# The first group of a two-level MLP product: two products of the second group taken into it, and buffers and steps moved to make room

## The chip, the cores and the metric

The kernel runs on one core of one Trainium2 chip. The metric is the device time of one execution in microseconds (us). A core has five engines that each work through their own list of instructions in order: TensorE (PE, matmuls and their weight loads), VectorE (DVE), ScalarE (ACT), GpSimd (POOL, here mostly a queue that issues DMAs) and SyncE (SP, a queue that issues DMAs). They meet at semaphores only: an instruction whose operand is not ready stands at the head of its engine's list, and all that is behind it waits too. Matmul results land in PSUM, eight banks of 128 x 512 float32; everything else lives in SBUF, in rooms that pools hand out by tag.

## The reference

One block of a hybrid encoder on a sequence of 512 rows and 2048 columns, in float32:

```python
h = rmsnorm(x, norm_mix_pre);  proj = h @ w_in                      # 2048 x 5120
mix = concat(pool_mixer(proj[:, :1024]), hgrn2(proj[:, 1024:])) @ w_out
x = x + rmsnorm(mix, norm_mix_post)
h = rmsnorm(x, norm_mlp_pre)
ff = square(relu(h @ w_mlp_in)) @ w_mlp_out                         # 2048 x 8192, 8192 x 2048
out = x + rmsnorm(ff, norm_mlp_post)
```

## The kernel before, in words

**Float32 by halves.** Every float32 operand is split in two: a high half that ACT writes by a cast, and a low half, which is the operand minus the high half and which DVE writes. A product is then three matmuls: high by high, high by low, low by high. A weight tile of 512 x 512 (one DMA of 1 MB) is split in two pieces of 128 x 1024 each, on ACT (line 863, results named `mh`) and DVE (line 864, `ml`). An operand of the activations is split the same way (`split_in`, lines 895 and 896, results named `a`).

**Stages.** The input projection (`pj`, ten groups of four units) with the pooling and the recurrence between its matmuls; the out projection (`om`, four groups); the first MLP product; the second MLP product. In the projection's first group, the sum of squares of x is turned into a row `rbc` that scales every result: DVE writes a diagonal tile `rb_dg`, PE spreads it by one matmul (`rb_ps`, line 129), ACT copies it (line 130), and then the results of the group can leave their banks.

**The first MLP product** takes 2 x 2 blocks by seven products in place of eight (numbered 1 to 7, done in the order 1, 2, 5, 3, 6, 7, 4). `slots` lists (group, product, half): eight groups of 1024 columns, seven products, two halves of the depth, so 112 slots. Each slot multiplies one weight tile (split while the slot before runs) with one activation operand. Products 5, 3, 6 and 7 need sums of activation blocks (`s1`, `s2`, `s3`, `s7`, line 899) before their operands can be split. The operands are kept for all groups, so only the first group, slots 0 to 13, makes them, and it does so while it runs: transposing the out projection's rows on PE (`feed_in`, result `fps`, moved out of PSUM on ACT at line 924 or on DVE at line 928), forming sums and splitting. The table `plan` says which of these steps stand ahead of a slot's matmuls and which in their middle. The rows themselves come from the out projection: `residual_task` scales a tile of 128 rows, adds x (line 779) and stores it, and `norm2_task` (lines 791 to 802) squares it for the second norm. A little clock (`clock.tick`, once per block or slot) runs such tasks after a count of ticks.

The first group runs *narrow*: 48 matmuls of 256 columns per slot, in single banks (`mi`, line 1035), since four of the eight banks serve the transposes. Later groups run *wide*: 16 matmuls of 512 columns (high and low operand side by side, line 1020) and 16 of 256 (line 1023), in `ps`.

**Weights.** Product 1, 5, 6 and 4 use a tile X, product 2, 3 and 7 a tile YZ; after a split the next tile is added onto the old one by an accumulating DMA on POOL (line 870), or a new one is loaded by SP (lines 847 and 853). `YZ0` takes the room that the norm weight `wpost` held during the out projection.

Lines of the loop that set the order in a slot:

```python
w_split_all(k + 1)
for f in before:
    f()
clock.tick()
products_in(k, hook)
evac_in(k, 1)
```

The split of the next slot's weight thus stands first in the lists of ACT and DVE, and the operand splits of the plan behind it.

## Time and profile before

| | us |
|---|---|
| median of 3 runs (lowest, highest) | 1971.12 (1970.82, 1973.6) |
| the profiled execution: time, span | 1971.38, 1969.7 |
| PE busy | 1944.2 |
| DVE busy | 1286.0 |
| ACT busy | 837.7 |
| input projection's first 100 us: PE without work from 20 to 100 us | 1.0 |
| first MLP group, slots 0 to 13, by the first and the last matmul's start | 699.3 to 798.0 |
| PE without work from 699.3 to 757.2 us | 7.5 |
| granted PE clock from 748.1 to 754.3 us | 0.50 |

The profile gives, for each engine, when an instruction began, how long it took and what ended the wait ahead of it. Starts matter more than durations: the duration of a matmul or of a DVE step overlaps the next one, so the pace is the distance between starts. PE counts as busy while a matmul is in its pipeline; whether it runs at full speed is told by the granted clock alone.

### The profile page before, as it was taken

The numbers are of one execution on the slowest core, as the hardware profiler recorded it, in microseconds if no ns is written. First come the engines' busy times: TensorE is split into PE (matmuls) and PEld (weight loads), VectorE is DVE, ScalarE is ACT, GpSimd is POOL, SyncE is SP. The second block draws the span as 40 slices with busy tenths as digits, with TensorE's granted clock in tenths as the row PEclk, the third lists the DMA queues.
The fourth block names the chain that finished last, engine by engine and source line by source line (L and its number), as shares of the span: only waits on it lengthen the run. The fifth ranks groups of instructions, "written<-read, shape, count | busy, mean of one in ns | idle before, by whom it ended". The sixth has DMA issues, their size and how long they took to land.

```text
span 1969.7 us, 24368 instructions
## 1 busy us (share of the span) xinstructions
PE 1944.2 (99%) x10008; PEld 1657.4 (84%) x10008; DVE 1286.0 (65%) x1420; ACT 837.7 (43%) x1000; POOL 145.1 (7%) x227
## 2 busy tenths in 40 slices
PE   9999999999999999999999999999999999999996
PEld 7888888888888889988888888888888888888885
DVE  5647443754632387566765766677778878878877
ACT  6222232223232275444444444445544444444454
POOL 1000000000000010111111011011010010010110
PEclk9999999999999999999999999999999999999998
DMA  7231222211343377889889888898897897897896
GB/s 310 86 107 65 86 69 103 86 65 65 118 192 107 118 206 193 214 216 220 213 213 216 229 210 211 223 241 245 209 251 222 200 236 229 210 227 219 219 227 134
DMA packets 56063, 354.98 MB, mean 180 GB/s; under 512 B 6032, under 2 KB 7056, under 8 KB 18064
## 3 DMA queue, kind: packets, MB, share of 16 engines
q0 software_dynamic: 24912, 162.54, 39.4%
q1 hardware_dynamic: 30752, 190.37, 26.5%
q8 instruction: 78, 1.28, 0.2%
q10 hardware_dynamic: 288, 0.52, 0.1%
q14 instruction: 33, 0.27, 0.0%
HBM read 328.24 MB, written 25.17 MB: 179 GB/s over the span
## 4 chain that ended last, share of the span: by engine, by line
PE 93%; DVE 2%; ACT 2%; DMA 1%; issue 1%; SPq 0%; DVEq 0%; ACTq 0%
PE pj L243 20%; PE ps L1020 18%; PE al L1236 17%; PE ga L1236 13%; PE ps L1023 10%; PE om L243 9%; PE mi L1035 3%; PE lps L610 2%; DMA xt<-in_x_t 1%; DVE ml L864 1%; DMA wr<-in_w_in 0%; ACT xrow L405 0%; ACT mh L863 0%; PE po L673 0%; DVE a L896 0%
## 5 line engine op out<-in xcount | busy, mean ns | idle before, releaser
L1020 PE MATMUL ps<-a,mh 128*128 128x512 f32 x1568 | 378.4, 391 | 0.0
L1020 PEld LDWEIGHTS ps<-a,mh 128*128 128x128 f32 x1568 | 286.7, 188 | 54.9 <-issue 0.3
L1236 PE MATMUL al<-mh,o 128*128 128x512 f32 x1024 | 316.9, 389 | 0.0
L863 ACT CAST mh<-X 128x1024 fp32r<-128x1024 f32 x176 | 180.2, 1053 | 209.7 <-PE ps L1020 87.5
L863 ACT CAST mh<-YX 128x1024 fp32r<-128x1024 f32 x176 | 180.5, 1054 | 157.4 <-PE al L1236 44.6
L864 DVE TENSOR_TENSOR ml<-X,mh 128x1024 fp32r<-128x1024 f32 x176 | 207.4, 1220 | 57.7 <-ACT mh L863 57.4
L1236 PE MATMUL ga<-mh,o 128*128 128x512 f32 x768 | 237.7, 389 | 0.0
L243 PE MATMUL pj<-xT,wh 128*128 128x512 f32 x760 | 236.2, 392 | 0.0
L864 DVE TENSOR_TENSOR ml<-YX,mh 128x1024 fp32r<-128x1024 f32 x176 | 207.4, 1220 | 35.2 <-ACT mh L863 35.1
L1236 PEld LDWEIGHTS al<-mh,o 128*128 128x128 f32 x1024 | 192.2, 188 | 40.1 <-ACT mh L863 0.3
L202 DVE TENSOR_TENSOR wl<-wr,wh 128x1024 fp32r<-128x1024 f32 (+1 forms) x118 | 136.5, 1168 | 131.3 <-ACT wh L201 131.2
L1023 PEld LDWEIGHTS ps<-a,ml 128*128 128x128 f32 x1568 | 203.8, 191 | 9.3
L1023 PE MATMUL ps<-a,ml 128*128 128x256 f32 x1568 | 206.7, 283 | 0.0
L1236 PE MATMUL al<-ml,o 128*128 128x512 f32 x512 | 199.5, 390 | 1.1 <-DVE ml L864 1.0
L201 ACT CAST wh<-wr 128x1024 fp32r<-128x1024 f32 (+1 forms) x118 | 116.0, 1003 | 155.4 <-PE pj L243 73.0
L1236 PEld LDWEIGHTS ga<-mh,o 128*128 128x128 f32 x768 | 144.1, 188 | 29.9
L243 PE MATMUL pj<-wh,xT 128*128 128x512 f32 x512 | 168.9, 397 | 0.0
L243 PEld LDWEIGHTS pj<-xT,wh 128*128 128x128 f32 x760 | 141.5, 188 | 29.1 <-issue 0.5
L863 ACT CAST mh<-YZ 128x1024 fp32r<-128x1024 f32 x96 | 98.4, 1052 | 124.2 <-PE ps L1020 54.8
L1236 PE MATMUL ga<-ml,o 128*128 128x512 f32 x384 | 149.4, 389 | 0.0
L1072 DVE TENSOR_TENSOR t<-t,ps 128x512 f32<-128x512 f32 x126 | 86.6, 687 | 94.7 <-ACT t L1075 71.8
L243 PE MATMUL pj<-xT,wl 128*128 128x512 f32 x380 | 148.1, 390 | 0.0
(212 smaller groups left out, 2503.0 us busy)
## 6 DMA issues: line engine op xcount, KB each, us to landing
wr<-in_w_in SPq DMA_DIRECT2D x38, 1024.0 KB, 4.8
X<-in_w_mlp_in POOLq DMA_DIRECT2D x33, 1024.0 KB, 9.2
X<-in_w_mlp_out POOLq DMA_DIRECT2D x33, 1024.0 KB, 9.8
YX<-in_w_mlp_in POOLq DMA_DIRECT2D x23, 1024.0 KB, 9.8
YX<-in_w_mlp_out POOLq DMA_DIRECT2D x23, 1024.0 KB, 9.6
YX<-in_w_mlp_in SPq DMA_DIRECT2D x21, 1024.0 KB, 5.6
YX<-in_w_mlp_out SPq DMA_DIRECT2D x21, 1024.0 KB, 4.9
wr<-in_w_out SPq DMA_DIRECT2D x16, 1024.0 KB, 4.8
```

Source lines behind the costliest of these rows:

```text
L201: nc.scalar.copy(out=hi[:, ks, :], in_=raw[:, ks, :])
L202: nc.vector.tensor_tensor(out=lo[:, ks, :], in0=raw[:, ks, :], in1=hi[:, ks, :].bitcast(F32), op=ALU.subtract)
L243: nc.tensor.matmul(bank, l, r, start=first and kt == 0 and oi == 0, stop=last and kt == 3 and oi == 2)
L610: nc.tensor.matmul(ps[r:r + mb, h, w, b0:b1], K[:, h, w * P + r:w * P + r + mb], rhs[:, b0:b1, 1, :], start=True, stop=True)
L863: nc.scalar.copy(out=hi[:, ks, :], in_=raw[:, ks, :])
L864: nc.vector.tensor_tensor(out=lo[:, ks, :], in0=raw[:, ks, :], in1=hi[:, ks, :].bitcast(F32), op=ALU.subtract)
L1020: nc.tensor.matmul(o, hi[:, kt, ms], r, start=first and kt == 0, stop=q == 1 and kt == 3 and not first, skip_group_check=True)
L1023: nc.tensor.matmul(o[:, 0], lo[:, kt, ms], r[:, 0], start=False, stop=q == 1 and kt == 3, skip_group_check=True)
L1035: nc.tensor.matmul(o, l[:, kt, ms], r[:, x], start=st and oi == 0 and m % 2 == 0, stop=sp and oi == 2, skip_group_check=True)
L1072: nc.vector.tensor_tensor(out=t, in0=t, in1=half(banks, s_), op=sign)
L1236: nc.tensor.matmul(bank[h] if type(bank) is list else bank[:, h, :], a[:, l, kt, ts], r[:, kt, :], start=i in (1, 2, 5) and kt == 0 and oi ...
```

## The change

Seven edits:

1. **Slots.** Product 2 of group 1 (two slots, one for each half) is done within the first group's run, right after product 2 of group 0: it uses the same operand `a2`. The narrow stage has 16 slots (`n_first`), and group 1 goes on later without its product 2. The result stands in two banks of the transposes' pool (`PM`, names `pm`), is copied out by ACT in slot 10 (`keep_pm`) into a room `tnext`, and product 1 of group 1 is added to it.
2. **Plan.** All transposes are moved out on ACT but one (rows 0 to 255, columns 512 to 1023), which is fed within the out projection now, on DVE; the sums, splits and `norm2_task` are spread over slots 0 to 12; the squares go in pairs.
3. **Order in a slot.** Operand steps of the plan come ahead of the next weight's split.
4. **Residual.** Row tiles 2 and 3 start four and three ticks later, and their second half follows after one tick.
5. **YZ0** has a room of its own from the start of the out projection, and its first load is issued in the last group of it; `wpost` lies in two rooms of the pool of results (`tmp`, four rooms where there were three).
6. **Scratch.** The scratch tile `junk` moves from a pool of two rooms to the recurrence's pool (two rooms) and then to one room; masks and small constants of the mixer move to that pool as well.
7. **First group of the projection.** Its `rb_ps` matmul and first evictions come after the third block, where they came after the second.

```diff
-                if feeder and ui == n - 1 and j < 2:
-                    if j:
+                if feeder and ui == n - 1 and j < 3:
+                    if j == 2:
                         next(nb, None)
-                        evac(0, banks[0])
-                        evac(1, banks[1])
+                        for jj in range(3):
+                            evac(jj, banks[jj])
...
+        YZ[0] = tp2.tile([P, 4, 512], F32, tag="big", bufs=1, name="YZ0")
+        late["wpost"] = [tp2.tile([P, 1024], F32, tag="tmp", bufs=4, name=f"wpost{h}") for h in range(2)]
...
-                clock.add(residual_task(t), 0)
+                clock.add(residual_task(t), (0, 0, 4, 3)[t])
...
-    slots = [(g, i, q) for g in range(2 * NP) for i in ORDER for q in range(2)]
+    order = [(0, 1), (0, 2), (1, 2)] + [(0, i) for i in ORDER[2:]] + [(1, i) for i in ORDER if i != 2]
+    order += [(g, i) for g in range(2, 2 * NP) for i in ORDER]
+    slots = [(g, i, q) for g, i in order for q in range(2)]
+    n_first = 16
...
     def during_mix(j, k):
-        if (j, k) == (2, 1):
+        if (j, k) == (0, 0):
+            load_yz(0)
+        elif (j, k) == (2, 1):
...
             feed_in(1, 0, "act")
+            feed_in(1, 1, "dve")
             split_in(1, 0, raw_in(1, 1, 0))
...
     plan = {
-        0: ([feed_step(1, 1, "act"), spl(1, 1, 1, 1)], [feed_step(1, 2, "dve")]),
-        1: ([lambda: new_act(2), spl(2, 0, 1, 2)], [feed_step(1, 3, "act"), lambda: clock.add(norm2_task(), 0)]),
-        2: ([spl(2, 1, 1, 2), feed_step(2, 0, "dve")], [feed_step(2, 2, "act"), s7(0)]),
-        3: ([lambda: new_act(5), s1(0), spl(5, 0, 2, 1), feed_step(2, 1, "dve")], [feed_step(2, 3, "act"), s7(1)]),
-        4: ([s1(1), spl(5, 1, 2, 1), lambda: new_act(4), spl(4, 0, 2, 2)], [s2(0), s3(0)]),
...
+        0: ([spl(1, 1, 1, 1)], [feed_step(1, 2, "act"), feed_step(1, 3, "act")]),
+        1: ([lambda: new_act(2), spl(2, 0, 1, 2)], []),
+        2: ([spl(2, 1, 1, 2)], [feed_step(2, 0, "act")]),
+        3: ([feed_step(2, 1, "act")],
+            [feed_step(2, 2, "act"), s7(0), s7(1), lambda: clock.add(norm2_task(), 0)]),
+        4: ([feed_step(2, 3, "act"), new_pm, s1(0)], []),
+        5: ([s1(1), lambda: new_act(5), spl(5, 0, 2, 1), lambda: new_act(4), spl(4, 0, 2, 2)], []),
+        6: ([spl(5, 1, 2, 1), s2(0), spl(4, 1, 2, 2)], []),
+        7: ([s3(0), lambda: new_act(3, yp, "Y"), spl(3, 0, 1, 2), s2(1)], []),
+        8: ([s3(1), spl(3, 1, 1, 2)], []),
+        9: ([lambda: new_act(6, yp, "Y"), spl(6, 0, 2, 2, True)], []),
+        10: ([spl(6, 1, 2, 2, True)], [keep_pm]),
...
-        main = PA if i in (1, 6, 7, 4) else PG
+        main = PA if i in (1, 6, 7, 4) else PG if k >= n_first or g == 0 else PM
...
-        w_split_all(k + 1)
         for f in before:
             f()
+        w_split_all(k + 1)
```

How this moves instructions at three places. In PE's list, the end of the projection's first group (`pj` with its bank's number, `rb_ps` the spread norm). Before:

```order
L243 MATMUL pj_1_198<-xT_154,wh_369 128x512 x2
L243 MATMUL pj_1_198<-xT_154,wl_370 128x512
L129 MATMUL rb_ps<-rb_dg,ones 128x512
L243 MATMUL pj_2_199<-xT_154,wh_369 128x512 x2
L243 MATMUL pj_2_199<-xT_154,wl_370 128x512
```

and now:

```order
L251 MATMUL pj_2_199<-xT_157,wh_369 128x512 x2
L251 MATMUL pj_2_199<-xT_157,wl_370 128x512
L138 MATMUL rb_ps<-rb_dg,ones 128x512
L251 MATMUL pj_3_200<-xT_157,wh_369 128x512 x2
L251 MATMUL pj_3_200<-xT_157,wl_370 128x512
```

The spread norm stands one block of twelve matmuls later. In DVE's list, from the split of slot 1's weight on (`ml_...<-X`), the first operands (`a`), residual rows (`Y<-Y,rt,xr`), transposes moved out by DVE (`RU<-fps`) and weight splits. Before:

```order
L864 TENSOR_TENSOR ml_4600<-X_4526,mh_4599 128x1024 x2
L896 TENSOR_TENSOR a_4531<-YX,a_4531 128x1024
L928 TENSOR_TENSOR RU<-fps,vec 128x512 x2
L864 TENSOR_TENSOR ml_4561<-YZ_4597,mh_4560 128x1024 x2
L896 TENSOR_TENSOR a_4691<-RU,a_4691 128x1024
L779 SCALAR_TENSOR_TENSOR Y_3721<-Y_3721,rt,xr_4024 128x512 x2
L864 TENSOR_TENSOR ml_4600<-YX,mh_4599 128x1024 x2
L896 TENSOR_TENSOR a_4691<-RU,a_4691 128x1024
L928 TENSOR_TENSOR RU<-fps,vec 128x512 x2
```

and now, from the second operand of slot 1 on:

```order
L916 TENSOR_TENSOR a_4524<-YX,a_4524 128x1024
L884 TENSOR_TENSOR ml_4588<-X_4519,mh_4587 128x1024 x2
L771 TENSOR_REDUCE sst<-ss_m 128x1
L129 TENSOR_SCALAR msq<-sst 128x1
L774 RECIPROCAL rt_y<-rt_y 128x1
L775 SCALAR_TENSOR_TENSOR rt<-rt_y,msq 128x1
L776 SCALAR_TENSOR_TENSOR rt<-rt,rt_y 128x1
L789 SCALAR_TENSOR_TENSOR Y_3721<-Y_3721,rt,xr_4028 128x512 x2
L916 TENSOR_TENSOR a_4688<-RU,a_4688 128x1024
L884 TENSOR_TENSOR ml_4566<-YZ_3722,mh_4565 128x1024 x2
```

The operand stands ahead of the weight split that shares its slot, the transposes are gone from DVE here, and the residual of tile 2 stands behind slot 1's weight. In DVE's list around products 5, 4, 3 and 6, where sums (`RU<-RU,A`, `A<-A,YX`), operands and weight splits alternate. Before:

```order
L864 TENSOR_TENSOR ml_4600<-X_4526,mh_4599 128x1024 x2
L899 TENSOR_TENSOR RU<-RU,A_4907 128x1024
L896 TENSOR_TENSOR a_4858<-RU,a_4858 128x1024
L896 TENSOR_TENSOR a_4956<-A_4813,a_4956 128x1024
L899 TENSOR_TENSOR A_4813<-A_4813,YX 128x1024
L899 TENSOR_TENSOR RU<-RU,A_4813 128x1024
L864 TENSOR_TENSOR ml_4561<-YZ_4597,mh_4560 128x1024 x2
L892 SCALAR_TENSOR_TENSOR a_5022<-A_4813,a_5022 128x1024
L896 TENSOR_TENSOR a_5025<-RU,a_5025 128x1024
```

and now:

```order
L884 TENSOR_TENSOR ml_4588<-YX,mh_4587 128x1024 x2
L919 TENSOR_TENSOR RU<-RU,A_4920 128x1024
L916 TENSOR_TENSOR a_5000<-RU,a_5000 128x1024
L916 TENSOR_TENSOR a_5003<-A_4878,a_5003 128x1024
L884 TENSOR_TENSOR ml_4566<-X_4397,mh_4565 128x1024 x2
L916 TENSOR_TENSOR a_5000<-RU,a_5000 128x1024
L919 TENSOR_TENSOR A_4878<-A_4878,YX 128x1024
L916 TENSOR_TENSOR a_5003<-A_4920,a_5003 128x1024
L884 TENSOR_TENSOR ml_4588<-X_4519,mh_4587 128x1024 x2
L919 TENSOR_TENSOR RU<-RU,A_4878 128x1024
L916 TENSOR_TENSOR a_5126<-RU,a_5126 128x1024
```

Between two weight splits there are now at most three operand steps, where there were five, and the operands of products 3 and 6 come behind one more pair of weight splits.

In SP's list the first load of `YZ0` stands between the loads of X0 and X1 in the out projection; it stood behind the loads of X0, X1 and YX. On PE, two feeds of transposes stand in the middle of slot 0 now.

More of the change, by code (lines that the diff above doesn't have):

```diff
@@ L65, in hybrid_block, with junk_tile @@
     pss = pss_pool.__enter__()
+    hg = tc.tile_pool(name="hg", bufs=1)
+    hgp = hg.__enter__()
+    late = {}
+    def junk_tile(shape, name):
+        if "tp2" in late:
+            return late["tp2"].tile(shape, F32, tag="junk", bufs=1, name=name)
+        return hgp.tile(shape, F32, tag="junk", bufs=2, name=name)
     x2_dram = dram.tile([T, D], F32, name="x2_dram")
@@ L88, in hybrid_block @@
     for w in (2, 4, 8, 16):
[L89 removed]
+        e = hgp.tile([P, w], F32, name=f"edge{w}")
         for c in range(w):
@@ L122, in row_bcast @@
     def row_bcast(dst, col):
-        dg = small.tile([P, NT, P], F32, tag="junk", name="rb_dg")
+        dg = junk_tile([P, NT, P], "rb_dg")
         nc.vector.tensor_tensor(out=dg, in0=ident.unsqueeze(1).to_broadcast([P, NT, P]),
@@ L215, in hybrid_block @@
     unit_no = [0]
-    late = {}
     def take_unit():
@@ L564, in col_products @@
             def col_products(i, a, b):
-                pr = small.tile([P, 512], F32, tag="junk", name="pr")
+                pr = junk_tile([P, 512], "pr")
                 nc.vector.tensor_tensor(out=pr.rearrange("p (h x) -> p h x", h=a.shape[1]), in0=a, in1=b, op=ALU.mult)
@@ L750, in late_pools @@
         late["Y"] = [ys[t // 2][:, t % 2, :] for t in range(NT)]
-        late["wpost"] = tp2.tile([P, D], F32, tag="big", bufs=1, name="wpost")
-        nc.gpsimd.dma_start(late["wpost"], norm_mix_post[0:1, :].broadcast_to([P, D]))
-        nc.scalar.mul(late["wpost"], late["wpost"], -0.5)
+        YZ[0] = tp2.tile([P, 4, 512], F32, tag="big", bufs=1, name="YZ0")
+        late["wpost"] = [tp2.tile([P, 1024], F32, tag="tmp", bufs=4, name=f"wpost{h}") for h in range(2)]
+        for h, wp in enumerate(late["wpost"]):
+            nc.gpsimd.dma_start(wp, norm_mix_post[0:1, h * 1024:(h + 1) * 1024].broadcast_to([P, 1024]))
+            nc.scalar.mul(wp, wp, -0.5)
     def row_rstd(t):
@@ L786, in residual_task, with row_square @@
             row_square(t)
-    def row_square(t):
-        for u in range(4):
-            junk = small.tile([P, 512], F32, tag="junk", name="junk")
+    def row_square(t, us=range(4)):
+        for u in us:
+            junk = junk_tile([P, 512], "junk")
             nc.scalar.activation(out=junk, in_=late["Y"][t][:, u * 512:(u + 1) * 512], func=AF.Square,
@@ L816, in f @@
             yv = late["Y"][t][:, n * 512:(n + 1) * 512]
-            junk = small.tile([P, 512], F32, tag="junk", name="junk")
+            junk = junk_tile([P, 512], "junk")
             nc.scalar.activation(out=junk, in_=bank, func=AF.Square, accum_out=ss_m[:, t, n:n + 1])
-            nc.vector.tensor_tensor(out=yv, in0=bank, in1=late["wpost"][:, n * 512:(n + 1) * 512], op=ALU.mult)
+            nc.vector.tensor_tensor(out=yv, in0=bank, in1=late["wpost"][n // 2][:, n % 2 * 512:n % 2 * 512 + 512],
+                                    op=ALU.mult)
             if n == 3:
-                clock.add(residual_task(t), 0)
+                clock.add(residual_task(t), (0, 0, 4, 3)[t])
         return f
@@ L959, in hybrid_block @@
     tp2, yp = late["tp2"], late["yp"]
-    YZ[0] = tp2.tile([P, 4, 512], F32, tag="big", bufs=1, name="YZ0")
-    load_yz(0)
     HI[1] = wspl.tile([P, 4, 512], F32R, tag="hi", name="mh1")
@@ L1061, in evac_in @@
         g, i, q = slots[k]
-        if q == 0:
+        wide = k >= n_first
+        if q == 0 or (not wide and g):
             return
@@ L1070, in add @@
             t = tmp[j][:, 2 * h:2 * h + 2]
-            for s_ in (parts if g else (None,)):
+            for s_ in (parts if wide else (None,)):
                 nc.vector.tensor_tensor(out=t, in0=t, in1=half(banks, s_), op=sign)
         def take(j, banks):
-            nc.scalar.copy(out=tmp[j][:, 2 * h:2 * h + 2], in_=half(banks, 0 if g else None))
-            if g:
+            nc.scalar.copy(out=tmp[j][:, 2 * h:2 * h + 2], in_=half(banks, 0 if wide else None))
+            if wide:
                 add(j, banks, parts=(1,))
+        kept = i == 1 and "next" in tmp
         if h == 0 and i in (1, 5, 6, 4):
-            new_tmp(i)
-        if i == 1:
+            if kept:
+                tmp[1] = tmp["next"]
+            else:
+                new_tmp(i)
+        if kept:
+            add(1, PA)
+        elif i == 1:
             take(1, PA)
@@ L1089, in evac_in @@
             t = tmp[6][:, 2 * h:2 * h + 2]
-            nc.vector.tensor_tensor(out=t, in0=half(PG, 0 if g else None), in1=t, op=ALU.subtract)
-            if g:
+            nc.vector.tensor_tensor(out=t, in0=half(PG, 0 if wide else None), in1=t, op=ALU.subtract)
+            if wide:
                 add(6, PG, parts=(1,))
@@ L1105, in evac_in @@
                 ends.append(finish_in(4, 2, 2 * g))
+            if kept:
+                del tmp["next"]
     ends = []
@@ L1268, in rest @@
                     t = 2 * tp - 2 + h
-                    junk = small.tile([P, 512], F32, tag="junk", name="junk")
+                    junk = junk_tile([P, 512], "junk")
                     nc.scalar.activation(out=junk, in_=yv[:, h], func=AF.Square, accum_out=ss_m[:, t, n:n + 1])
```

74 lines of the change are left out of this document (41 added, 33 removed).

## The prediction, made before the run

> **What bounds the kernel now.** I read the busy shares first, then the table by stretches of time, then PE's own list where it had no work.
>
> ```profile
> PE 1944.2 (99%) x10008; PEld 1657.4 (84%) x10008; DVE 1286.0 (65%) x1420; ACT 837.7 (43%) x1000; POOL 145.1 (7%) x227
> ...
> 20.00:100.00 80.00, 79.01 (x347) 64.75 (x346) 45.76 (x65) 34.78 (x51) 0.00 (x0) 1.00 0.43 166
> 100.00:600.00 500.00, 500.00 (x2593) 419.32 (x2592) 254.51 (x349) 133.50 (x168) 2.98 (x6) 1.00 0.27 96
> ...
> 699.30:757.20 57.90, 50.39 (x390) 48.98 (x388) 51.26 (x62) 41.36 (x75) 6.37 (x8) 0.94 0.73 184
> 757.20:798.00 40.80, 40.80 (x339) 40.55 (x338) 24.95 (x24) 19.68 (x23) 4.30 (x6) 1.00 0.85 235
> 748.10:754.30 6.20, 6.20 (x29) 6.20 (x30) 6.03 (x9) 4.57 (x6) 0.00 (x0) 0.50 0.68 140
> ```
>
> Columns: stretch, length, busy time of PE, PEld, DVE, ACT, POOL, granted PE clock, DMA share, GB/s. PE is the bound nearly everywhere: from 100 to 600 us it has no idle time. Only order and waits on PE can be won, and PE lacks work at three places: 0.99 us in the first 100, 7.5 of 57.9 in the first ten slots of the MLP, and the tail, which the change doesn't touch. In those ten slots DVE is busy 51.26 of 57.9 us, the highest share of any engine: there DVE sets the pace. Behind it PE ran at half clock for 6.2 us.
>
> ```profile
> 699.34 0.48 PE L1035 MATMUL mi<-a,mh 128*128 128x256 f32 x2
> 707.15 0.38 PE L1035 MATMUL mi<-a,mh 128*128 128x256 f32 x1 [0.95 <-ACT a L895]
> 708.41 0.38 PE L1035 MATMUL mi<-a,mh 128*128 128x256 f32 x1 [0.88 <-DVE a L896]
> 731.28 0.48 PE L1035 MATMUL mi<-a,mh 128*128 128x256 f32 x2 [1.16 <-DVE t L1072]
> 738.85 0.39 PE L1035 MATMUL mi<-a,mh 128*128 128x256 f32 x1 [0.88 <-DVE a L896]
> 748.04 0.80 PE L1035 MATMUL mi<-a,mh 128*128 128x256 f32 x2 [3.31 <-ACT t L1075]
> ...
> 757.65 40.31 PE mi L1035 x336
> 797.96 1.84 PE ps L1020 x8
> 855.52 1.91 PE ps L1023 x16
> 857.44 3.65 PE ps L1020 x16
> 861.09 1.91 PE ps L1023 x16
> ```
>
> The waits are for operands of slots 1, 5 and others, each made by a cast on ACT and a subtraction on DVE that stand behind a weight split; the last one is a bank that ACT copies late. The last five rows, from the chain that ended last, give PE's pace: 40.31 / 336 = 0.120 us for a narrow matmul, so 5.76 for a slot of 48; a wide slot repeats every 861.09 - 855.52 = 5.57 us.
>
> **The change part by part.** *First MLP group.* What PE must do from 699.34 to 797.96 (98.62 us): 14 slots x 5.76 = 80.6; six feeds of transposes; the spread norm, at most 1.0, say 0.9.
>
> ```profile
> 698.55 1.03 PE L919 MATMUL fps<-ident,Y 128*128 128x128 f32 x8
> ...
> 740.86 1.98 ACT L863 CAST mh<-YZ 128x1024 fp32r<-128x1024 f32 x2
> 742.74 1.06 ACT L891 ACTIVATE a<-A 128x1024 fp32r<-128x1024 f32 x1
> 738.39 0.63 ACT L791 ACTIVATE junk<-Y 128x512 f32<-128x512 f32 x1
> 738.92 0.19 ACT L791 ACTIVATION_READ_ACCUMULATOR junk<-Y 128x1 f32 x1
> 739.01 0.62 ACT L791 ACTIVATE junk<-Y 128x512 f32<-128x512 f32 x1
> 707.88 2.00 ACT L863 CAST mh<-YZ 128x1024 fp32r<-128x1024 f32 x2 [0.78 <-DMA YZ<-in_w_mlp_in]
> ...
> 742.37 2.35 DVE L864 TENSOR_TENSOR ml<-YZ,mh 128x1024 fp32r<-128x1024 f32 x2
> 744.64 1.22 DVE L892 SCALAR_TENSOR_TENSOR a<-A,a 128x1024 fp32r<-128x1024 f32 x1
> 745.78 1.22 DVE L896 TENSOR_TENSOR a<-RU,a 128x1024 fp32r<-128x1024 f32 x1
> 708.27 1.28 DVE L928 TENSOR_TENSOR RU<-fps,vec 128x512 f32<-128x512 f32 x2
> 709.47 2.35 DVE L864 TENSOR_TENSOR ml<-YZ,mh 128x1024 fp32r<-128x1024 f32 x2
> 712.87 1.41 DVE L779 SCALAR_TENSOR_TENSOR Y<-Y,rt,xr 128x512 f32<-128x512 f32 x2
> 693.19 0.69 DVE L819 TENSOR_TENSOR Y<-om,wpost 128x512 f32<-128x512 f32 x1 [1.00 <-ACT junk L818]
> ...
> L129 PE MATMUL rb_ps<-rb_dg,ones 128*128 128x512 f32 x2 | 1.0, 592 | 0.0
> ```
>
> A feed costs PE 699.34 - 698.55 = 0.79 and a slower restart, say 0.87; six are 5.2. Together 86.7, so 11.9 us are lost now: to the waits, to half speed (6.2 x about 0.45 = 2.8) and to refilling the pipeline. After the change, the feed that stood ahead of slot 0 stands in the out projection, which costs as much there, so slot 0 begins at 699.3 as before; the stage has 16 slots: 92.2 + 5.2 + 0.9 = 98.3 us plus its own waits W. It contains two slots that took 2 x 5.57 = 11.1 later. Gain: 98.6 + 11.1 - 98.3 - W = 11.4 - W; the two slots are 2 x 0.19 = 0.4 dearer narrow than wide, which is in it.
>
> [...]
>
> *W by a walk* through the new lists with distances between starts from the rows above: DVE 2.27 for a weight's low halves, 1.14 for an operand's or a sum (1.25 where the next step reads it), 1.32 for two residual pieces, 1.20 for a feed; ACT 1.88 for a weight, 0.96 for an operand, 0.62 for a square. It starts at the eviction of row tile 2 at 693.19 and stands on the old time axis. The DVE work per narrow slot is the point. Two new slots bring DVE only two weight splits (4.5 us, no operand, as `a2` is there) against 11.5 us of PE work, and three feeds fewer on DVE less one new save 2.4: the same ten slots' work on DVE now stands beside twelve slots of PE.
>
> - Slot 1: operand at 702.5, weight at 704.8, PE comes at 706.7: no wait, where it lost 2.2 us (708.41 against the 706.15 of an unbroken run).
> - Slot 2: weight at 713.0, PE needs its second half at 713.4. In its middle the transposes want row tile 3, whose residual now stands behind slot 2's weight: ready 716.15, PE at 715.3: **0.85**.
> - Slots 3 to 5: weights at 720.3, 725.8, 733.1; PE at 720.7, 728.1, 733.8: none. From here the lead is used up.
> - Slots 6 and 7: low halves complete at 739.8 and 746.1, needed 0.96 into slots that begin at 739.6 and 745.3: none, by 0.1 to 0.7.
> - Slot 8: PE at 751.05, the weight's first low half and the copy of `t5` out of its bank at 752.0: **1.15** with the second half.
> - Slot 9: **0.1**. After it lead grows: operand and weight of slot 10 at 762.6, PE at 763.8.
>
> W = 2.1. Two costs aren't in the trace. With one scratch room each square waits for the one before: between nothing (from start to start the rows show 0.62 with two rooms) and a whole accumulator read, 0.19, exposed in the ten that stand ahead of the casts for slots 6 to 9, 2.0; I take 0.7, nearer to nothing, since in the rows a square already starts only when that read is half over. The second loads of YZ0 and YX can be issued only when slots 2 and 3 have been split (713.0 and 720.3) and are cast at 722.4 and 729.7, 9.4 us later:
>
> ```profile
> DMA to landing us min/median/max: 6.4/7.3/11.1
> YX<-in_w_mlp_in SPq DMA_DIRECT2D x1, 1024.0 KB, 8.6
> ```
>
> By 8.6 they are in time, at 11.1 the YX one pushes slot 6 by 1.6; I take nothing. The accumulating loads on POOL have over 10 us of lead, and the bank copies (`keep_pm`) stand where ACT has room, before slot 11. So W = 2.8, gain 8.6; bounds W = 0 and W = 6.4 (2.1 + 2.0 + 1.6 and 0.7 for what the walk rounds): gain 11.4 to 5.0.
>
> *First group of the projection.*
>
> ```profile
> 43.91 0.39 PE L243 MATMUL pj<-xT,wl 128*128 128x512 f32 x1
> 44.59 0.39 PE L243 MATMUL pj<-xT,wl 128*128 128x512 f32 x1
> 45.97 1.13 PE L129 MATMUL rb_ps<-rb_dg,ones 128*128 128x512 f32 x2 [0.99 <-DVE rb_dg L125]
> 45.22 0.69 DVE L125 TENSOR_TENSOR rb_dg<-ident,rstd 128x512 f32<-128x512 f32 x1
> ```
>
> PE could have gone on at 44.59 + 0.23 = 44.8 and waits to 45.97. With a block of 2.7 us in between, the diagonal (done 45.9) is there first: 1.1 us won. What is late next: the copy of `rbc` and three evictions, now at 48.9 to 51.8; the next group wants its first bank at 50.9 and has it at 50.6. Cover 0.3 us; if it goes, the gain shrinks toward 0.5. I take 1.0.
>
> *The rest at nothing.* `YZ0` earlier: its load now goes out before X1's and is there long before 707.88; the 0.78 us that ACT waited for it is inside the 11.9 counted above. The two-room `wpost`: the same bytes and ACT work, long before use. Masks in another pool: same steps, same order. In the tail only one square in a pair gains a wait, beside weight casts.
>
> Sum: 8.6 + 1.0 = 9.6 on the profiled 1971.38 (0.26 above the median): 1961.8; against the median 1971.12, 1961.5.
>
> **Rivals.** *A, the operand chain stays the bound.* Slots 5 to 8 have 22.0 us of DVE steps, and twice a sum goes DVE, ACT, DVE with 1.1 us of waiting: 24.2 against 23.0 of PE. If casts or loads come 1 us late at each of four slots, W = 7 to 9, gain 3.5 to 5.5: 1967. For it: those slots' margins are 0.1 to 0.7 us. Against: a short list, without transposes or long runs of sums.
>
> *B, the clock drops again.* In the MLP the half clock came once, behind the 3.31 us wait, and not behind the ones of about 1. If one wait of slots 6 to 9 still reaches 3.3, it costs 3.3 + 2.8 = 6.1: gain 9.6 - 6.1 + 1 = 4.5 or less, 1967 to 1970. Against it: the cause, a bank copy that stood behind the second norm's chain on ACT, is gone; that chain now stands five slots later than the copy. [...]
>
> *C, slower.* B's mechanism several times over: the second loads of YZ0 and YX land late behind the two stores of the residual and the two accumulating loads, and each leaves PE idle past 3.3 us. It needs landings beyond 9.4 + 3.3 + the lead of 2 or so, 15 us, in both, and again on the sum chain; two drops (12.2) leave it within 0.2%, from the third on it is slower: 3 x 6.1 = 18.3 less 9.6, 1980. Against: 11.1 is the longest seen.
>
> *D, it doesn't do what it says.* PE's waits only move: slots 0 to 9 run at DVE's old pace and the two slots add theirs. Gain then only the head's 1.0 and what the clock gives: 1969.
>
> **How the numbers follow.** Forecast (gain 6.5 to 12.5) 0.74; A 0.12; B 0.06; D 0.04; C 0.04. No change means within 0.2%, 3.9 us, about what a measurement here can tell. Faster: the forecast, most of A, a third of B: 0.87; same 0.09; slower 0.04. Range: low end all waits gone, 11.4 + 1.1 below the median, 1958.6, rounded down to 1958.2; high end through A's middle, 1967.0.
>
> **What would show it.** Right: the first wide matmul between 797 and 801 us (the head's gain of 1.0 included) with 16 narrow slots ahead of it; no stretch at half clock there; PE's idle time ahead of `mi` matmuls 1 to 4 us, in slots 2 and 8; no idle time ahead of `rb_ps` at 45 us. Wrong: waits for `a` or `ml` in slots 5 to 9 above 1 us each; a wait of ACT for a YX load near 730; a granted clock of 0.5; a wait for a bank at 51 us.

## The result, and the profile after

The changed kernel takes 1961.6 us (median of 4 runs, 1961.2 to 1962.29) against 1971.03 (4 runs, 1970.82 to 1973.6) on the same chip: a ratio of 0.995, interval 0.9932 to 0.9967. The forecast was 1961.5. The profiled execution took 1961.64 with a span of 1959.9, against 1971.38 and 1969.7 before.

First the busy times of the page of the changed kernel, and its table by stretches (columns as in the prediction):

```profile
PE 1941.4 (99%) x10040; PEld 1656.5 (85%) x10040; DVE 1281.7 (65%) x1414; ACT 841.9 (43%) x1009; POOL 146.2 (7%) x228
...
20.00:100.00 80.00, 80.00 (x352) 65.58 (x351) 46.12 (x65) 35.66 (x52) 0.00 (x0) 1.00 0.43 167
...
698.00:757.00 59.00, 58.16 (x481) 57.48 (x480) 49.91 (x57) 45.96 (x81) 5.54 (x7) 1.00 0.71 184
```

In the first ten to twelve slots of the MLP, PE idles 59.00 - 58.16 = 0.84 us, where it idled 7.5, and the granted clock is 1.00 where it was 0.94. DVE is busy nearly as long as before (49.9 of 59 us, 51.3 of 57.9 before), but PE no longer waits for it. The whole idle time stands in one row of PE's timeline, ahead of slot 8; the chain that ended last shows the end of the narrow slots:

```profile
699.80 0.40 PE L1074 MATMUL mi<-a,mh 128*128 128x256 f32 x2
...
752.20 0.51 PE L1074 MATMUL mi<-a,mh 128*128 128x256 f32 x2 [0.84 <-ACT t L1111]
```
```profile
752.20 17.54 PE mi L1074 x144
769.74 0.86 PE rb_ps L138 x2
770.60 28.79 PE mi L1074 x240
799.39 1.84 PE ps L1059 x8
```

From slot 0 at 699.80 to the first wide matmul at 799.39 are 99.59 us with 16 slots, where 98.62 held 14. The two slots now missing later took 2 x 5.57 = 11.14. Gain of the stage: 98.62 + 11.14 - 99.59 = 10.2 us. The span fell by only 9.8: slot 0 begins at 699.80 instead of 699.34, although the wait of 0.99 us ahead of `rb_ps` is gone. So the MLP brought more than the forecast 8.6, and what lies ahead of it cost 0.46 where a gain of 1.0 was forecast. That second part was the first thing to be explained.

### The profile page after: what moved, and what is told of

The parts are those of the page before. It is cut to its first block, busy times and chain, and to the rows that moved or that the text cites. A ratio compares the mean times of both kernels' runs of the same rounds, so it can differ in the third digit from the quotient of the medians.

```text
span 1959.9 us, 24431 instructions
## 1 busy us (share of the span) xinstructions
PE 1941.4 (99%) x10040; PEld 1656.5 (85%) x10040; DVE 1281.7 (65%) x1414; ACT 841.9 (43%) x1009; POOL 146.2 (7%) x228
## 4 chain that ended last, share of the span: by engine, by line
PE 96%; DVE 1%; ACT 1%; issue 0%; DMA 0%; SPq 0%; DVEq 0%; ACTq 0%
PE pj L251 22%; PE ps L1059 18%; PE al L1280 17%; PE ga L1280 13%; PE ps L1062 9%; PE om L251 9%; PE mi L1074 4%; PE lps L616 2%; ACT mh L883 0%; DVE ml L884 0%; PE po L679 0%; PE fps L939 0%; DMA wr<-in_w_in 0%; PE po L681 0%; PE kvps L661 0%
## 5 line engine op out<-in xcount | busy, mean ns | idle before, releaser
L1059 PE MATMUL ps<-a,mh 128*128 128x512 f32 x1536 | 370.6, 391 | 0.0
L1059 PEld LDWEIGHTS ps<-a,mh 128*128 128x128 f32 x1536 | 281.0, 188 | 53.6 <-issue 0.3
L1062 PEld LDWEIGHTS ps<-a,ml 128*128 128x128 f32 x1536 | 199.6, 191 | 9.0
L1062 PE MATMUL ps<-a,ml 128*128 128x256 f32 x1536 | 202.4, 283 | 0.0
L1108 DVE TENSOR_TENSOR t<-t,ps 128x512 f32<-128x512 f32 x120 | 82.5, 687 | 88.6 <-ACT t L1111 67.4
```

The source lines that it names most:

```text
L1059: nc.tensor.matmul(o, hi[:, kt, ms], r, start=first and kt == 0, stop=q == 1 and kt == 3 and not first, skip_group_check=True)
L1062: nc.tensor.matmul(o[:, 0], lo[:, kt, ms], r[:, 0], start=False, stop=q == 1 and kt == 3, skip_group_check=True)
L1108: nc.vector.tensor_tensor(out=t, in0=t, in1=half(banks, s_), op=sign)
```

## Experiments

Beside the totals, each trace gives two marks: the start of slot 0, and the first wide matmul (here by its own row in PE's timeline, 797.79 before, 0.17 ahead of the chain's figure). The last column shows that nothing but the two slots changes behind the stage, split_first apart.

| kernel | slot 0 | first wide | stage (slots) | behind it | median us |
|---|---|---|---|---|---|
| before | 699.34 | 797.79 | 98.45 (14) | 1171.9 | 1971.0 to 1972.2 |
| head_only | 698.59 | 795.90 | 97.31 (14) | 1171.8 | 1970.34 |
| late_norm | 699.97 | 797.91 | 97.94 (14) | 1171.9 | 1973.29 |
| no_two_slots | 699.57 | 796.24 | 96.67 (14) | 1171.9 | 1969.66 |
| changed | 699.80 | 799.23 | 99.43 (16) | 1160.7 | 1961.6 |
| repeat | 699.25 | 798.66 | 99.41 (16) | 1160.6 | 1960.92 |
| no_head | 701.29 | 800.75 | 99.46 (16) | 1160.9 | 1963.12 |
| split_first | 699.55 | 800.57 | 101.02 (16) | 1162.1 | 1963.20 |
| dve_feeds | 698.94 | 799.14 | 100.20 (16) | 1160.7 | 1961.95 |
| better | 699.37 | 797.76 | 98.39 (16) | 1160.7 | 1960.13 |
| wait1 | 699.60 | 799.79 | 100.19 (16) | 1160.7 | 1962.47 |
| wait2 | 699.41 | 801.85 | 102.44 (16) | 1160.7 | 1964.42 |
| wait4 | 699.18 | 803.98 | 104.80 (16) | 1160.7 | 1966.26 |
| pad1024 | 699.07 | 798.50 | 99.43 (16) | 1160.7 | 1961.09 |

(The runs come from three chips. Beside them the kernel before took 1971.98 (repeat, head_only, no_head, better), 1972.16 (late_norm, no_two_slots, split_first, dve_feeds) and 1971.87 (the wait kernels and pad1024), so totals from different chips can be compared to about 0.3 us.)

### What was lost ahead of slot 0: repeat, head_only, no_head

**repeat**, nothing edited:

> The changed kernel once more, nothing edited. In its first profile the fourth weight piece of the start came late (PE waits 0.73 us at 9.94), so that from 11 to 44 us all stood about 1.1 us later than in the kernel before, and slot 0 of the MLP began at 699.80 instead of 699.34 although the wait ahead of the diagonal matmuls (1.0 us) was gone. Theory 'chance': the late piece belongs to that one execution; here the first projection matmuls start like those of the kernel before (no wait near 9.9 us), slot 0 begins near 698.8 and the profiled time is about 1 us lower, 1960.6. Rival 'systematic': the pools that were moved ahead change the start; the same wait of 0.7 us stands there again and slot 0 begins at 699.8. In both the MLP from slot 0 to the first wide matmul takes 99.6 us with one wait of 0.8 us in slot 8.

1960.92 us (1960.62 to 1961.07), 0.9945 of the kernel before, interval 0.9932 to 0.9957; slot 0 at 699.25. The late start is not a part of the program: the same program starts earlier here. Whether it differs from one execution to the next, or with the chip and the time of measuring, these runs don't separate: all four runs of the first comparison (1961.2 to 1962.29) lie above all five here. PE's timeline of the first changed profile, then of the repeat:

```profile
9.94 0.73 PE L251 MATMUL pj<-xT,wh 128*128 128x512 f32 x2 [0.73 <-ACT wh L210]
...
48.42 1.02 PE L138 MATMUL rb_ps<-rb_dg,ones 128*128 128x512 f32 x2
```
```profile
6.32 2.14 PE L238 MATMUL pj<-xT,wh 128*128 128x512 f32 x8 [0.62 <-ACT wh L210]
...
47.29 1.02 PE L138 MATMUL rb_ps<-rb_dg,ones 128*128 128x512 f32 x2
51.36 0.73 PE L251 MATMUL pj<-xT,wh 128*128 128x512 f32 x2 [0.29 <-DVE pu L452]
```

The same program reaches `rb_ps` 1.13 us earlier, since no weight piece is late at 9.94. But slot 0 comes only 0.55 earlier: with PE early, the wait for a bank at 51 us appears that the prediction named as its wrong sign. It is 0.29 us, and the matmuls around it are slow to follow; at 58.3 us, where the first changed profile stands at the same matmul at 58.84, the lead is down to 0.54.

**head_only**, the kernel before with this one edit:

```diff
-                if feeder and ui == n - 1 and j < 2:
-                    if j:
+                if feeder and ui == n - 1 and j < 3:
+                    if j == 2:
                         next(nb, None)
-                        evac(0, banks[0])
-                        evac(1, banks[1])
+                        for jj in range(3):
+                            evac(jj, banks[jj])
```

> The kernel before with the head's edit alone (the diagonal matmuls of the first norm after the third block of the last input unit, three evictions behind them). Theory: the wait of 0.99 us ahead of rb_ps is gone and nothing takes its place: 1.0 us less, 1970.0, slot 0 at 698.3. Rival: the wait comes back as a wait for a bank at 51 us or further on, or is eaten by a slower pace behind it: 1970.7 to 1971.2, slot 0 at 699.0 to 699.4.

1970.34 us (1968.8 to 1972.87, 11 runs), ratio 0.9993, interval 0.9984 to 1.0002: by time undecided, since both kernels spread over 3 to 4 us. The traces decide. Three instructions of the kernel before, of head_only and of the repeat: on PE the first matmul of the pooling product (`pps`), on VectorE a step at 93 us that waits for PE, and one near the end of the out projection:

```profile
66.02 0.39 PE L504 MATMUL pps<-pd,ps 128*128 128x512 f32 x1
...
93.42 0.69 DVE L525 TENSOR_TENSOR F<-pj,rbc 128x512 f32<-128x512 f32 x1 [8.79 <-PE pj L243]
...
687.69 0.69 DVE L819 TENSOR_TENSOR Y<-om,wpost 128x512 f32<-128x512 f32 x1 [0.93 <-ACT junk L818]
```
```profile
65.27 0.39 PE L504 MATMUL pps<-pd,ps 128*128 128x512 f32 x1
...
92.67 0.69 DVE L525 TENSOR_TENSOR F<-pj,rbc 128x512 f32<-128x512 f32 x1 [8.79 <-PE pj L243]
...
686.94 0.69 DVE L819 TENSOR_TENSOR Y<-om,wpost 128x512 f32<-128x512 f32 x1 [0.94 <-ACT junk L818]
```
```profile
65.11 0.39 PE L510 MATMUL pps<-pd,ps 128*128 128x512 f32 x1
...
92.84 0.69 DVE L531 TENSOR_TENSOR F<-pj,rbc 128x512 f32<-128x512 f32 x1 [8.83 <-PE pj L251]
...
687.58 0.69 DVE L832 TENSOR_TENSOR Y<-om,wpost 128x512 f32<-128x512 f32 x1 [0.99 <-ACT junk L831]
```

head_only is 0.75 ahead at all three: what the head's edit wins is kept to the MLP. Its start was 0.51 later than that of the kernel before (`rb_ps` at 48.05, less 12 matmuls of 0.227 = 45.33, against 44.59 + 0.23 = 44.82), so the edit itself won 1.26. (Its stage is 1.1 shorter as well, 97.31 against 98.45: behind the same wait, 3.29 against 3.31 us, the half clock lasted one stretch in this profile, 747.79 to 751.20 us, and two in that of the kernel before, 747.48 to 754.30. The section on the half clock tells why the two can differ.) The repeat is 0.91, 0.58 and 0.11 ahead: it loses 0.80 on the same code. That is the subject of pad1024.

**no_head**, the same edit taken back out of the changed kernel:

> The changed kernel with the head as it was before (diagonal matmuls after the second block). Theory: a wait of 1.0 us is back near 45 us and everything behind it moves: 1962.6, 1.0 above the changed kernel of the same chip. Rival (the head's edit brings nothing in the total): 1961.6.

1963.12 us (1962.87 to 1963.38), 2.2 above the repeat on the same chip. Of it the edit explains about half:

```profile
45.87 0.39 PE L251 MATMUL pj<-xT,wl 128*128 128x512 f32 x1
47.09 1.13 PE L138 MATMUL rb_ps<-rb_dg,ones 128*128 128x512 f32 x2 [0.82 <-DVE rb_dg L134]
```

The wait is back, 0.82. The start of this profile is late as well (PE had done the second block at 46.10; the first changed profile, by its `rb_ps` less 12 matmuls, at 45.70). Against that profile no_head stands 1.50 later at the first `pps` matmul (67.15 against 65.65); less 0.40 of start, 1.1 for the edit. So the head is worth 1.1 to 1.3 where the start is late, and less where it is early, by the wait for a bank: in the repeat 0.7 (0.91 ahead at `pps`, 0.25 of it from the start). That the late start of this one profile fills the rest of the 2.2 in all five runs is not shown.

### Where the matmuls lose 0.8 us: pad1024

```diff
+    pad = const.tile([P, 256], F32, name="pad")
+    nc.gpsimd.memset(pad[:, 0:1], 0.0)
     ident = const.tile([P, P], F32, name="ident")
```

> The changed kernel with 1024 more bytes per partition at the head of the constants, so that all later pools lie 1024 bytes higher; no other instruction than one memset of a column changes. Between the first projection group (59 us) and the end of the out projection (687 us) the profiles of the changed kernel lose 0.42 us against the kernel before on the same instructions, at the same places each time, while the kernel before with the head's edit alone loses 0.00. Theory 'place': the matmuls' pace hangs on where their operands lie, and with other addresses the loss comes at other places or in another size (0 to 0.8): the total moves by less than 0.5. Rival: the loss has another cause in the change and stays at 0.42 at the same places.

1961.09 us (1960.88 to 1962.59), the same as the changed kernel. It loses as much as the repeat, at the same places, so 1024 bytes move nothing and the rival's expectation holds; only its 0.42 is too small. That figure was taken from an instruction of VectorE at 59 us, which in the repeat does not wait for PE and so hides part of PE's lead. Read on PE, from the first `pps` matmul to 687 us, the first changed profile, the repeat and pad1024 all lose 0.80 to 0.81, and so do the other kernels built on the change (the three wait kernels 1.12 to 1.13), where head_only and late_norm lose nothing.

Three quarters of it are lost in two stretches, where the matmuls of the pooling product stand between those of the projections. From the first to the last `pps` matmul of the first stretch, the kernel before takes 13.38 us and the repeat 13.67:

```profile
79.40 0.39 PE L506 MATMUL pps<-pd,ps 128*128 128x512 f32 x1
```
```profile
78.78 0.39 PE L512 MATMUL pps<-pd,ps 128*128 128x512 f32 x1
```

The second stretch, in the out projection, gives 13.37 and 13.67, and all eleven kernels built on the change show the same 13.67 in both. Within it, while no DMA runs, with the same work on every engine and the clock at 1.00, PE's timeline before has

```profile
542.61 0.39 PE L243 MATMUL om<-wh,mh 128*128 128x512 f32 x1
...
546.69 0.39 PE L243 MATMUL om<-wh,mh 128*128 128x512 f32 x1
```

and in the repeat

```profile
542.23 0.40 PE L251 MATMUL om<-wh,mh 128*128 128x512 f32 x1
...
546.40 0.40 PE L251 MATMUL om<-wh,mh 128*128 128x512 f32 x1
```

for the same 18 matmuls: 4.08 against 4.17 us, 0.227 against 0.232 each. So the granted clock alone does not tell whether PE runs at its full pace, as the account of the profile before has it. Up to there the two programs differ in the head, which head_only clears, and in where tiles lie (all pools 6144 bytes lower, masks and scratch among the recurrence's tiles). The three wait kernels below, whose later pools lie 32 bytes off because of a small extra tile, differ from the changed kernel ahead of slot 7 in that alone, and lose 0.31 more. That points to place, but which tile and which rule was not found.

### What the two slots are worth: no_two_slots, late_norm

**late_norm**, the kernel before with one tick moved:

```diff
-        clock.tick()
+        if k != 5:
+            clock.tick()
         products_in(k, hook)
         evac_in(k, 1)
+        if k == 5:
+            clock.tick()
```

> The kernel before with one tick moved: the chain of the second norm (square root on ScalarE, spread of the diagonal on VectorE) is issued at the end of slot 5 instead of ahead of it, so that both copies of t5 out of their bank stand ahead of it on ScalarE. Theory: the wait of 3.31 us at slot 6 and the half clock behind it (6.2 us at half speed, 2.8 lost) are gone: up to 6.1 less, 1966 to 1967, the granted clock 1.0 there, and, since the length of the half-clock stretch can no longer differ, times within 1 us of each other where the kernel before spreads over 3 us. Rival: the operands of slots 5 to 7 are late anyway and the wait comes back under another name: 1969 to 1971.

1973.29 us (1971.9 to 1974.81), ratio 1.0008, interval 0.9999 to 1.0017: nothing won, the rival was right. PE's waits by line in the MLP:

```profile
PE mi L1035 <- DVE a L896: 3.3, 3, 1.6
PE mi L1035 <- ACT t L1075: 1.8, 1, 1.8
PE mi L1035 <- ACT a L895: 1.3, 2, 0.9
PE mi L1035 <- DVE t L1072: 1.2, 1, 1.2
```

The copy of `t5` still comes 1.8 late, since ScalarE waits 1.2 us ahead of it for a step of VectorE on another operand; then the norm's steps on VectorE stand ahead of the operands of slot 7 (1.6), while `rb_ps` itself runs at 754.91 without a wait. So the 3.3 us come back as 1.8 and 1.6. The clock drops here too (0.50 from 748.75 to 752.10 us), behind a wait of only 1.8. The norm's chain in the profile before was the last thing to arrive, not the cause. What fits both profiles is that VectorE had no time for the operands of ten slots beside ten slots of PE.

**no_two_slots**, the changed kernel with the order of the groups as before:

```diff
-    order = [(0, 1), (0, 2), (1, 2)] + [(0, i) for i in ORDER[2:]] + [(1, i) for i in ORDER if i != 2]
-    order += [(g, i) for g in range(2, 2 * NP) for i in ORDER]
+    order = [(g, i) for g in range(2 * NP) for i in ORDER]
-    n_first = 16
+    n_first = 14
...
+        2: ([spl(2, 1, 1, 2), feed_step(2, 0, "act")], [feed_step(2, 2, "act"), s7(0)]),
+        3: ([lambda: new_act(5), s1(0), spl(5, 0, 2, 1), feed_step(2, 1, "act")], [feed_step(2, 3, "act"), s7(1)]),
+        4: ([s1(1), spl(5, 1, 2, 1), lambda: new_act(4), spl(4, 0, 2, 2)], [s2(0), s3(0)]),
```

(The rest of the list, the residual's delays and the second norm as before, its chain behind `t5` as in late_norm.)

> The changed kernel without the two slots of the second group (14 narrow slots, the order of the groups as before, the second norm at the time it had before, but with its chain behind the copies of t5 as in the run above, so that no 3.3 us wait comes from there). The feeds on ScalarE, the operands ahead of the weight splits, the head and the pools stay as in the change. Theory 'cover': ten slots' work on VectorE stands beside ten slots of TensorE again, and waits of 3 to 6 us in all come back ahead of slots 4 to 8: 1964 to 1967. Rival 'the list': what gained was the order of the steps and the missing half clock, and the two slots add little: 1961 to 1962.5.

1969.66 us (1969.08 to 1971.62), ratio 0.999, interval 0.9982 to 0.9999. All the other edits together win 1.8 us in the stage (98.45 - 96.67); with the two slots it is 96.67 + 11.2 - 99.43 = 8.4 more. PE's waits:

```profile
PE mi L1066 <- DVE ml L880: 2.4, 5, 1.1
PE mi L1066 <- ACT junk L801: 2.2, 1, 2.2
PE rb_ps L138 <- DVE rb_dg L134: 0.7, 1, 0.7
PE mi L1066 <- ACT mh L879: 0.5, 1, 0.5
```

The 2.2 us stand where the kernel before waited 1.16 (731.28 there); the row that fits the release is VectorE's sum out of the bank, 730.38 to 731.06, behind low halves that waited 1.17 for ScalarE, which does the feeds in this list. So about 1 us of the 8.4 belongs to the list I wrote for this run, and 1.5 of it (below) is one stretch of half clock. "The list" is refuted. Cover is worth about 6 us without these two, and the total lies above what the theory expected.

### The order within the slots: split_first, dve_feeds

**split_first**:

```diff
+        w_split_all(k + 1)
         for f in before:
             f()
-        w_split_all(k + 1)
```

> The changed kernel with the weight split of the next slot ahead of the operand steps in every slot (the order of the kernel before). Theory: an operand that is wanted in the next slot then ends 2.3 us later on VectorE, its first half of the weight earlier; where the lead is used up (slots 5 to 9) this costs about 1 us each: 3 to 4 us in all, 1964 to 1965, waits named after `a`. Rival: both are needed by the start of the slot, so that the order within a slot moves nothing: 1961 to 1962.

1963.20 us (1962.79 to 1964.39), 2.3 above the repeat: between the two. In the stage it costs 1.6, with a new wait of 0.87 for `a` ahead of slot 9 and a wait of 1.01 instead of 0.84 ahead of slot 8. Another 1.5 stand behind the stage. Of them 1.15 are lost between 816 and 826 us, where ScalarE begins a weight's cast only at 816.42, after 4.95 us of waiting for its load (811.61 and 3.47 in the repeat); 0.3 come after the last wide matmul, without a reason found.

**dve_feeds**, with `"dve"` instead of `"act"` in three feed steps, one each in the lists of slots 0, 2 and 3 (row tiles 0 and 1: u = 2; row tiles 2 and 3: u = 0 and u = 1). The expectation counts four, and so 4.8 us where three make about 3.7:

> The changed kernel with four of its feeds back on VectorE (row tiles' transposes evicted there with the gain, 1.2 us for each feed, instead of 1.57 us on ScalarE). Theory: VectorE gets 4.8 us more in slots 0 to 4, where the lead over TensorE is used up by slot 6; of these 3 to 4.8 us come out as waits of TensorE in slots 5 to 8: 1964 to 1966. Rival: VectorE's idle pieces there (0.5 to 1.5 us each, 5 us between 718 and 741) take them up: 1961 to 1962.

1961.95 us (1961.21 to 1962.39), the rival's case. The stage is 0.77 longer, nearly all of it at one place, where the transposes of row tile 3 wait for its residual:

```profile
PE mi L1074 <- ACT t L1111: 0.8, 1, 0.8
PE fps L939 <- DVE Y L789: 0.7, 1, 0.7
```

VectorE is busy for 52.9 us from 698 to 757 us, where it was 49.9; of that no more than the 0.77 comes out in the stage, and slot 8 waits no longer than before. Once the two slots are there, VectorE has time for these three feeds; the fourth was not tried.

### What half the clock costs, and when it comes: wait1, wait2, wait4

The extra work is squares on ScalarE of data that nobody reads, ahead of the copies of `t5`; n is 1, 2 or 4:

```diff
         clock.tick()
+        if k == 7:
+            for u in range(n):
+                junk = junk_tile([P, 512], "junk")
+                nc.scalar.activation(out=junk, in_=rbc, func=AF.Square, accum_out=xtra[:, u:u + 1])
         products_in(k, hook)
```

> The changed kernel with one more square on ScalarE ahead of t5's copies in slot 7 (0.75 us, of data that nobody reads after; the output stays as it is). The wait ahead of slot 8 grows from 0.84 to 1.6 us. Theory 'window', read from the half-clock stretches of the runs so far (each 3.2 to 3.4 us long, or twice that, and each behind 3.4 us in which TensorE was idle for more than half, 1.7 us): 1.6 us is too little, no half clock, 0.75 more than the changed kernel and as little spread: 1961.7. Rival 'single wait', as in the prediction: only a wait of 3.3 us drops the clock: the same for this run.

1962.47 us (1962.1 to 1963.11). Wait 1.58, no half clock; the stage grows by 0.76, as both expected. The total is 1.55 above the repeat: 0.35 more lie ahead of slot 0 in the profile, about the 0.31 by which this kernel's matmuls are slower still, and 0.4 are left over between executions.

> Two more squares: the wait ahead of slot 8 is 2.3 us. Theory 'window': whether 1.7 us of it fall into one window depends on where the windows lie, for about two placements in three they do: executions differ by 1.5 us (3.4 us at half speed), 1962.4 without and 1963.9 to 1965.5 with the half clock. Rival 'single wait' (3.3 us and more): never a half clock, 1962.4 with a spread below 0.5 us.

1964.42 us; the five runs are 1962.68, 1964.28, 1964.42, 1964.62 and 1965.49. Wait 2.33, and the clock drops in the profile. The run of 1962.68 fits the case without a drop, but has no profile.

> Four more squares: the wait ahead of slot 8 is 3.8 us. Theory 'window': the clock drops in every execution and comes back after one window of 3.4 us, or two where the wait reaches into the next one: 3.0 of wait + 1.5 or 3.0 = 1965.4 to 1967. Rival 'single wait' as the prediction priced it: a drop of 6.2 us each time, 3.0 + 2.8: 1966.7, without spread. No drop at all would be 1963.9.

1966.26 us (1965.39 to 1966.81). Wait 3.85, and the clock drops. The stages grow by 3.0 and 5.4 us, where the waits grew by 1.5 and 3.0. "Window" is right, "single wait" refuted. The table by stretches, for the stretch ahead of the drop and for those behind it, first no_two_slots, then wait2, then wait4 (third column PE's busy time, third from the end the clock):

```profile
737.06:740.47 3.41, 1.67 (x11) 1.13 (x9) 3.41 (x4) 3.35 (x7) 0.00 (x0) 1.00 0.25 50
740.47:743.70 3.23, 3.23 (x15) 3.23 (x16) 3.20 (x3) 2.85 (x6) 0.88 (x1) 0.50 0.46 63
```
```profile
750.90:754.30 3.40, 1.07 (x10) 0.95 (x9) 2.94 (x3) 3.25 (x9) 0.87 (x1) 1.00 0.70 145
754.30:757.72 3.42, 3.42 (x19) 3.42 (x18) 2.77 (x3) 3.39 (x6) 0.00 (x0) 0.50 1.00 163
```
```profile
749.75:753.16 3.41, 1.02 (x9) 0.81 (x7) 3.41 (x4) 3.28 (x10) 0.41 (x1) 1.00 0.93 192
753.16:756.57 3.41, 1.96 (x9) 1.96 (x10) 0.97 (x2) 3.38 (x8) 0.46 (x1) 0.50 0.74 99
756.57:759.98 3.41, 3.41 (x18) 3.41 (x18) 2.95 (x3) 3.35 (x7) 0.16 (x1) 0.50 1.00 209
```

And in the kernel before:

```profile
744.08:747.48 3.40, 0.66 (x6) 0.46 (x4) 3.17 (x5) 0.82 (x3) 0.87 (x1) 1.00 0.38 39
747.48:750.89 3.41, 2.85 (x13) 2.85 (x14) 3.13 (x8) 3.41 (x6) 0.00 (x0) 0.50 0.94 192
750.89:754.30 3.41, 3.41 (x18) 3.41 (x18) 3.38 (x4) 1.78 (x3) 0.00 (x0) 0.50 0.38 77
```

Half clock began some time after PE had gone on again (wait2: PE runs from 753.35, the drop is at 754.3), lasted 3.4 us where PE was busy throughout (wait2 3.42, head_only 3.41), and a second time as long where PE still idled in the first (0.56 us in the kernel before, 1.45 in wait4). That is what windows of 3.41 us would give. The clock's records also fit windows that follow each other from the first change to the last: any two changes lie a whole number of them apart (in the kernel before, from 6.76 us on, 740.69 us at full clock, 6.83 at half and 1204.90 at full: 217, 2 and 353 times 3.413; in the changed kernel 1945.60 us at full clock: 570 times).

Idle times in the stretch ahead of a drop were 1.74 (no_two_slots), 1.92 (late_norm), 2.33 (wait2), 2.39 (wait4), 2.74 (the kernel before) and 2.91 us (head_only). The 1.58 of wait1 say nothing of the least: by its records a border between two windows lies at 751.78, inside the wait, which leaves 0.6 us in one and 1.0 in the next. But late_norm's wait of 1.57 lies within one window (755.53 to 758.94) and no drop followed, and near the end of the changed kernel and of the repeat, windows with 1.74 and 1.80 us without a matmul passed without one, too. So the least seen ahead of a drop is 1.74 us, about half of 3.41, with no sharp border in these profiles, and no single long wait was needed: in no_two_slots it was waits of 0.45 and 1.13 and short stops beside them.

The price is read from wait2's rows behind the drop:

```profile
754.69 0.63 PE L1074 MATMUL mi<-a,mh 128*128 128x256 f32 x2
755.11 0.41 PE L1074 MATMUL mi<-a,ml 128*128 128x256 f32 x1
755.33 0.63 PE L1074 MATMUL mi<-a,mh 128*128 128x256 f32 x2
```

Three matmuls in 0.64 us instead of 0.36: a stretch of 3.4 us does 16 instead of 28, and loses 1.5.

### Without the last wait: better

```diff
-        7: ([s3(0), lambda: new_act(3, yp, "Y"), spl(3, 0, 1, 2), s2(1)], [])
+        7: ([s3(0), s2(1), lambda: new_act(3, yp, "Y"), spl(3, 0, 1, 2)], [])
...
-        for t in (2, 3):
-            for h in range(2):
-                row_square(t, (2 * h, 2 * h + 1))
-                yield 1
+        row_square(2, (0, 1))
+        yield 1
+        row_square(2, (2, 3))
+        yield 2
+        row_square(3)
+        yield 1
```

> The changed kernel with two things moved around slot 7: the sum s2(1) on VectorE ahead of the operand's split, where VectorE waits 1.11 us for a cast, and no squares of the second norm in slot 7, so that the copies of t5 out of their bank stand straight behind the weight's casts (row tile 3's four squares go together one slot later). Theory: slot 8's first matmul waits neither for the copy nor for low halves: the 0.84 us is gone, 1960.8, MLP to the first wide matmul 98.7 us. Rival: the four squares delay the operand of slot 10 on ScalarE by 1.5 us and a wait of up to 1 us appears there: 1961.6 or a little more.

1960.13 us (1959.85 to 1960.91), 0.9941 of the kernel before, interval 0.9929 to 0.9954, and 0.8 below the repeat. The stage is 98.39, 1.0 shorter, and PE has no wait left in it. All its waits up to 1900 us (the last 58 us, which the change doesn't touch, have one more of 0.8):

```profile
PE warm_ps L391 <- POOL ones L83: 1.6, 1, 1.6
PE pj L251 <- DVE pu L452: 0.3, 1, 0.3
PE al L1282 <- DVE ml L886: 0.3, 1, 0.3
PE pj L238 <- ACT wh L210: 0.2, 1, 0.2
```

This version beats both kernels.

## Why the prediction was right, point by point

- **The term that carries it** (two slots bring VectorE little work and PE 11.5 us) is shown by no_two_slots: without them 8.4 of the stage's 10.2 us are gone. The stage ends at 799.39, inside the predicted 797 to 801.
- **W was taken as 2.8 and is 99.59 - 98.3 = 1.3.** This is the mis-sized step; it hid 1.5 us of gain. Slot 8 was right in place and cause (1.15 forecast, 0.84 found, for the copy of `t5`). Slot 2 was not: 0.85 forecast, but its transposes lost about 0.2 (eight took 1.19 us instead of 1.03). The walk let them wait for both pieces of the residual; they read the first 512 columns, and so only the first piece. With the feeds on VectorE a wait does appear there, 0.7. The squares do run apart by more with one scratch room (below), but of the 0.7 taken for it, by the order of the lists, only the two squares ahead of `t5`'s copies stand on PE's path.
- **The head's 1.0** is confirmed as the size of the edit (1.26 and 1.1), and so is its stated cover of 0.3: with PE early the bank wait comes, 0.29. It did not show in the first comparison because of two things that the sum did not have: a start that was late by 0.9 (45.70 against 44.82) in that execution, and 0.81 us of slower matmuls, which every kernel built on the change has. 0.88 - 1.26 + 0.81 = 0.43, about the 0.46 by which slot 0 came later.
- **"The rest at nothing"** is therefore wrong by 0.8 in one place. Beside the head, which head_only clears, the masks and scratch that were moved are the only edit up to the first of the two stretches, so tiles at other addresses were not free, though the mechanism is open.
- **Rival A** (operands stay the bound) did not come: the waits for `a` and `ml` in slots 5 to 9 are nil.
- **Rival B** did not come either, but its reading failed. The prediction tied the drop to one wait of 3.3 us. Runs with waits of 2.3 and 1.8 us drop the clock too, and no_two_slots with 1.74 us in pieces, so the margin from 0.84 was 0.9, not 2.5. And the "6.2 us, 2.8 lost" of the profile before were two stretches of 3.41 us (6.83 together by the clock's record); one clean stretch costs 1.5 us here, by wait2's rows.
- **"The cause is gone"** (the norm's chain ahead of the bank copy) was only argued. late_norm takes this cause away alone and wins nothing. What removed the waits was in the main the cover, by no_two_slots, in which the norm's chain also stands behind the copies and waits of 5.8 us are left.
- **C and D**: no late YX or YZ0 load held ScalarE, and PE's waits did not move elsewhere.

That the total agreed to 0.1 us is luck, since errors of opposite sign met: 1.5 more from W and 0.3 from the head, against 0.9 of late start and 0.8 of slower matmuls. In the repeat, without the late start, the same kernel takes 1960.9.

## What to carry to other kernels

When an engine beside the bound is full for a stretch, look for work of the bound that brings it none, and bring that in from later; taking away the one wait that shows only moves it, as long as that engine is full. Price waits by how much idle time falls together, not by the longest one, since here 1.74 us or more within 3.41 us stood ahead of every drop of the clock in the MLP, and a drop costs another 1.5 us. Measure PE's progress on PE's own instructions, or on steps that wait for them. And hold two executions of the same program against each other before a difference of one microsecond is put down to an edit.
